# Values turned by VectorE and DRAM instead of TensorE in one stage of a fp32 hybrid layer (1 core)

## The chip, the cores and the metric

One core of one Trainium2 chip runs the whole layer in one launch. The metric is the device time in microseconds (us), the median of the runs. Engines are TensorE (PE, with its weight loads PEld), VectorE (DVE), ScalarE (ACT), GpSimd (POOL) and SyncE (SP, which here only issues DMAs).

## What is computed

One layer on 2048 prompt frames and 8 x 16 sample frames, all in float32. Cut to what the change touches:

```python
h = rmsnorm(x, norm_mix_pre)
P = h @ w_in            # q|k|v (3*512) | z | b | a | B | C | H
qkv = silu(causal_dwconv(qkv_in, conv_prev, conv_qkv_w))
q = l2norm(q) * GDN_HEAD_DIM ** -0.5
k = l2norm(k)
A = strict_lower((k * beta) @ k.T * decay)          # chunks of 64, 4 heads of 128
sol = triangular_solve(eye + A, [v * beta, k * beta * exp(g)])
qk = lower(q @ k.T * decay)
o = ...                 # recurrence over chunks with state S
o = rmsnorm(o, gdn_norm_w) * silu(z)
y = B * causal_dwconv3(C * H)
x = x + rmsnorm(concat(o, y) @ w_o)
x = x + rmsnorm((silu(h @ w_gate) * (h @ w_up)) @ w_down)
```

## The kernel before

The program runs in stages. Stage 1 (0 to about 851 us) is the in-projection with convolution, delta rule and short convolution; then come the out-projection (L1200), gate and up (L1446) and down (L1637). The change lies in stage 1 alone.

Stage 1 takes 17 tiles of 128 rows in five groups: tiles 0 to 3, 4 to 7, 8 to 10, 11 and 12 with the sample tile, and 13 to 15. They are called group 0 to group 4 here ("two to five" in the words of the change are 1 to 4). Each group goes through 28 blocks of 128 output columns: k, v, q, z for four heads, then C, H, B for four slices. A block is 24 matmuls (L326: eight k-slices, each as hi times hi, lo times hi and hi times lo) into one of three `dbank` banks. Weights come block by block, 1 MB each, into one of three buffers; the loads stand in order on SP's queue (`fetch`).

TensorE's order is written by hand. A block has three **slots** (k-slices 0 to 2, 3 to 5, 6 and 7), so a group has 84, and a slot is 9, 9 or 6 matmuls. `plan` hangs all other work on slot numbers through `at(slot, function)`: `SEQS` is the order of the blocks, `PLAN` gives the slots of the decay, the pairs, the solve, the levels and the chunks, `TURNS` the slots of the turns. The other engines' order is made by a scheduler at build time from that program.

The work around the change, by head h and tile i of a group:

- `conv_qkv` evacuates a block, DVE adds three taps (L330), ACT takes silu, and the result stands transposed (head dimension on partitions, tokens along): kT, qT and vraw.
- `turned` (L384) turns it back by one TensorE transpose a tile into a `tbank`. k is copied to `kt` (L409), v is scaled by beta times the norm into `vt` (L427), and of q only the sum of squares is taken (`sumsq`: ACT squares, L389, DVE adds up, L390).
- `pair_keys` (L597) multiplies k by k into a `gbank`, and DVE multiplies that by the decay into AU (L598). `pair_queries` (L604, L605) does the same with q and k.
- `solve_load` copies the 32 x 32 diagonal blocks of AU to `pk` (ACT, L620), turns them to `As` (DVE, L622) and loads half a unit matrix to `Ts` (L612). `solve` then runs 31 dependent steps on DVE (L631, L633), and `solve_store` turns the solved blocks twice (L638 to `td`, L639 to `ud`).
- `level_a` (L650) begins on TensorE with `td`, and `level_b` (L671, L672) and `level_cd` (L699, L701) build the larger inverse; then `chunk` runs the recurrence, from L768 on.
- There are two `gbank` banks, so a matmul that opens one waits until DVE or ACT has emptied the last but one.

## Time and profile before

| | us |
|---|---|
| median of three runs | 2421.25 (2420.97 to 2421.59) |
| the profiled execution | 2421.49 |
| its span in the profile | 2419.5 |

The profile's page gives for the whole span: PE busy 2402.4 us (99%), DVE 1603.4 (66%), ACT 1064.3 (44%), POOL 561.3 (23%), TensorE's granted clock 0.999, DMA 561.36 MB at a mean of 232 GB/s. A table by stretches shows the part in question: between 260 and 850 us PE is busy for 588.7 of 590 us, DVE for 59 to 67 of every 100 us, the DMA engines for 0.58 to 0.76 of the time. Read the table against the page: the span is the time from the first to the last instruction, and the 2.0 us between it and the profiled execution's time lie around the program.

### The profile page before, as it was taken

What the parts mean: (1) busy time and instruction counts of PE and PEld (TensorE: products, weight loads), DVE (VectorE), ACT (ScalarE), POOL (GpSimd) and SP (SyncE); (2) the same over time, 40 slices, a digit from 0 to 9 for tenths busy, and PEclk for the clock granted to TensorE, in tenths of its full rate; (3) what the DMA queues carried; (4) which work ended last, traced back from release to release, by engine and by line L of the source; (5) the groups of instructions that cost most, each with busy time, mean ns of one, the idle gap of its engine ahead of it and who ended that gap; (6) DMA issues with size and microseconds to landing.
All of it is one profiled execution on the core that took longest, in us unless ns stands there. A gap on an engine that the chain in (4) does not pass through costs nothing.

```text
span 2419.5 us, 39078 instructions
## 1 busy us (share of the span) xinstructions
PE 2402.4 (99%) x14222; PEld 2204.9 (91%) x14222; DVE 1603.4 (66%) x3042; ACT 1064.3 (44%) x2367; POOL 561.3 (23%) x667
## 2 busy tenths in 40 slices
PE   9999999999999999999999999999999999999998
PEld 7888889999989988899999999999999988888877
DVE  7875755746667466888788744546456555666787
ACT  6645545546445445543444423334333345333443
POOL 1211001001110000256555200000000035455663
PEclk9999999999999999999999999999999999999999
DMA  8774655766777668599888888888988844334376
GB/s 289 259 245 170 221 192 195 251 216 240 259 260 248 243 177 240 208 339 296 271 280 267 287 254 254 256 261 271 311 297 282 253 154 129 101 120 127 118 235 205
DMA packets 317063, 561.36 MB, mean 232 GB/s; under 512 B 95940, under 2 KB 198536, under 8 KB 299592
## 3 DMA queue, kind: packets, MB, share of 16 engines
q1 hardware_dynamic: 216864, 490.66, 61.1%
q10 hardware_dynamic: 99784, 67.17, 9.0%
q8 instruction: 112, 1.84, 0.3%
q0 software_dynamic: 224, 1.05, 0.1%
q14 instruction: 79, 0.65, 0.1%
HBM read 400.09 MB, written 158.70 MB: 231 GB/s over the span
## 4 chain that ended last, share of the span: by engine, by line
PE 93%; DVE 3%; ACT 1%; DMA 1%; POOL 1%; issue 1%; POOLq 0%; SPq 0%; DVEq 0%; ACTq 0%
PE fbank L1446 36%; PE dbank L326 25%; PE fbank L1637 17%; PE dbank L1200 4%; PE ftbank L1200 4%; PE tbank L384 1%; PE gbank L597 1%; PE gbank L604 1%; PE obank L776 1%; PE gbank L768 1%; PE gbank L790 1%; PE obank L798 1%; PE gbank L784 1%; DVE sA L1413 0%; PE gbank L701 0%
## 5 line engine op out<-in xcount | busy, mean ns | idle before, releaser
L1446 PE MATMUL fbank<-xh,fw 128*128 128x384 f32 (+1 forms) x3696 | 898.2, 326 | 2.7 <-ACT m L1479 1.7
L1446 PEld LDWEIGHTS fbank<-xh,fw 128*128 128x128 f32 x3696 | 651.2, 188 | 5.0 <-ACT m L1478 2.7
L326 PE MATMUL dbank<-hi,w 128*128 128x384 f32 (+1 forms) x2224 | 650.8, 363 | 0.2 <-ACT w L1008 0.2
L1446 PE MATMUL fbank<-xl,fw 128*128 128x384 f32 (+1 forms) x1848 | 602.1, 326 | 0.0
L326 PEld LDWEIGHTS dbank<-hi,w 128*128 128x128 f32 x2224 | 409.6, 188 | 40.4 <-issue 4.5
L1637 PE MATMUL fbank<-dw,as 128*128 128x512 f32 x1785 | 416.1, 391 | 2.5 <-ACT as L1617 1.1
L1637 PEld LDWEIGHTS fbank<-dw,as 128*128 128x128 f32 x1785 | 334.6, 188 | 76.9 <-ACT as L1617 1.5
L326 PE MATMUL dbank<-lo,w 128*128 128x384 f32 (+1 forms) x1112 | 396.7, 357 | 0.3 <-DVE lo L241 0.3
L1446 PEld LDWEIGHTS fbank<-xl,fw 128*128 128x128 f32 x1848 | 346.9, 188 | 0.0
L326 PEld LDWEIGHTS dbank<-lo,w 128*128 128x128 f32 x1112 | 209.3, 188 | 16.0 <-DVE lo L241 0.6
L1620 POOL TENSOR_TENSOR as<-ar,as 128x256 fp32r<-128x256 f32 (+1 forms) x202 | 173.8, 869 | 182.3 <-ACT as L1617 170.4
L1617 ACT CAST as<-ar 128x256 fp32r<-128x256 f32 (+1 forms) x287 | 119.0, 427 | 203.1 <-PE fbank L1637 154.9
L1590 DVE TENSOR_TENSOR acc<-acc,fbank 128x512 f32<-128x512 f32 x219 | 148.0, 683 | 86.7 <-PE fbank L1637 68.5
L1285 POOL TENSOR_TENSOR dw<-dr,dw 128x512 fp32r<-128x512 f32 x48 | 67.7, 1418 | 513.8 <-ACT dw L1283 513.4
L1421 ACT CAST fw<-rg 128x512 fp32r<-128x512 f32 x124 | 77.2, 622 | 223.3 <-PE fbank L1446 136.8
L330 DVE SCALAR_TENSOR_TENSOR acc<-R,vec,acc 128x512 f32<-128x512 f32 (+2 forms) x180 | 120.8, 673 | 26.8 <-ACT acc L367 20.9
L1494 DVE TENSOR_TENSOR c<-u,fbank 128x384 f32<-128x384 f32 (+1 forms) x66 | 34.9, 528 | 98.1 <-PE fbank L1446 98.1
L1490 DVE TENSOR_TENSOR m<-m,m 128x384 f32<-128x384 f32 (+1 forms) x44 | 23.1, 526 | 81.3 <-ACT m L1480 81.2
L1497 ACT ACTIVATE c<-c 128x384 f32<-128x384 f32 (+1 forms) x66 | 33.4, 506 | 95.3 <-DVE c L1496 95.3
L1422 POOL TENSOR_TENSOR fw<-rg,fw 128x512 fp32r<-128x512 f32 x44 | 65.9, 1499 | 34.1 <-ACT fw L1421 34.0
L1492 ACT ACTIVATE m<-fbank 128x384 f32<-128x384 f32 (+1 forms) x66 | 31.2, 473 | 94.0 <-PE fbank L1446 70.2
L359 POOL COPY hist<-R 128x3 f32<-128x3 f32 x60 | 18.4, 307 | 217.9 <-ACT R L335 172.3
(402 smaller groups left out, 3558.2 us busy)
## 6 DMA issues: line engine op xcount, KB each, us to landing
w<-wsplit SPq DMA_DIRECT2D x105, 1024.0 KB, 5.1
fw<-fsplit SPq DMA_DIRECT2D x188, 512.0 KB, 4.8
fsplit<-fw SPq DMA_DIRECT2D x94, 512.0 KB, 4.3
partd<-pt ACTq DMA_DIRECT2D x86, 384.0 KB, 6.3
rg<-in_w_gu SPq DMA_DIRECT2D x62, 512.0 KB, 4.3
wsplit<-w SPq DMA_DIRECT2D x28, 1024.0 KB, 4.9
ar<-partd SPq DMA_DIRECT2D x43, 384.0 KB, 3.2
wr<-in_w_in SPq DMA_DIRECT2D x32, 512.0 KB, 6.2
```

Of the source, the lines that this page charges most:

```text
L326: T.matmul(ps[:, :c], l[:, k, :], r[k][:, :c], start=(k == 0 and r is hi and l is wh), stop=(k == KD - 1 and l is wl))
L330: r = V.scalar_tensor_tensor(acc, raw(d), w[:, d:d + 1], acc, op0=ALU.mult, op1=ALU.add)
L1200: T.matmul(pss[n], m_[:, j, :], w_[k][:, n * 512:(n + 1) * 512], start=(k == 0 and ci == 0), stop=(k == KD - 1 and ci == 2))
L1285: e.tensor_tensor(out=w[1], in0=v, in1=w[0].bitcast(F32), op=ALU.subtract)
L1421: A.copy(w[:, 0], v)
L1422: e.tensor_tensor(out=w[:, 1], in0=v, in1=w[:, 0].bitcast(F32), op=ALU.subtract)
L1446: T.matmul(ps, w_[:, c], b_[k][:, :hw], start=(first and k == 0 and ci == 0), stop=(k == KH - 1 and ci == 2), skip_group_check=not first)
L1494: V.tensor_add(c21, u2, b3)
L1590: mark_d["V"] = V.tensor_tensor(out=dst if out is None else out, in0=dst, in1=ps, op=ALU.add)
L1617: ins = mark_d["A"] = A.copy(a[:, 0, :n], v)
L1620: mark_d["V" if e is V else "G"] = e.tensor_tensor(out=a[:, 1, :n], in0=v, in1=a[:, 0, :n].bitcast(F32), op=ALU.subtract)
L1637: ins = T.matmul(ps, a[:, x_, q * P:(q + 1) * P], w[y_], start=(start and q == 0 and ci == 0), stop=(q == c - 1 and ci == 2), skip_group_c ...
```

## The change

For groups 1 to 4 (group 0 stays as it is):

1. **Values.** The TensorE transposes of v go. DVE transposes vraw within 32 x 32 blocks into `vt` (`turn`), four DMAs a head write it to DRAM in pieces of 128 bytes so that the blocks land where they belong (`turn_out`), one DMA a head reads it back in pieces of 512 bytes (`turn_in`), and ACT scales it in place (`value_scale`). All four have their own slots in `TURNS`.
2. **Queries.** The TensorE transposes of q go. DVE turns qT within 32 x 32 blocks, ACT squares, DVE adds up 32 columns at a time to four parts, and four small matmuls with 32 x 32 unit matrices (`eyes`) add the four parts (`query_sums`), which DVE copies out. The turn of q is held behind `leveled`, an instruction of `level_b`.
3. **Order.** The blocks go k, v, z, q instead of k, q, z, v; so `pair_queries` moves from slot 42 to 62 in group 1 and from 33 to 53 in the others. Its multiply is held behind `solved` (the second turn in `solve_store`). The chunks of group 1 begin at slot 68 instead of 66.
4. **Unit matrix.** The load of half a unit matrix moves 14 slots ahead.

```diff
@@ -37,17 +37,20 @@
 AX = mybir.AxisListType
 BLOCKS = [(kind, h) for kind in "kvqz" for h in range(H)] + [(kind, b) for b in range(4) for kind in "CHB"]
 SEQS = ([0, 12, 1, 13, 2, 14, 3, 15, 8, 16, 9, 17, 10, 4, 11, 5, 18, 6, 19, 7, *range(20, 28)],
-        [16, 17, 18, *range(0, 4), *range(8, 12), *range(12, 16), *range(4, 8), *range(19, 28)],
-        [*range(0, 4), *range(8, 12), *range(12, 16), *range(4, 8), *range(16, 28)])
+        [16, 17, 18, *range(0, 8), *range(12, 16), *range(8, 12), *range(19, 28)],
+        [*range(0, 8), *range(12, 16), *range(8, 12), *range(16, 28)])
 LATE = (*SEQS[0][:2], 7, 11, 19, 23, 27)
 PLAN = {0: (14, 20, 22, 26, 32, 36, 40, 50, (67, 69, 71), 75),
-        1: (16, 20, 23, 28, 26, 33, 38, 51, (56, 58, 60), 66),
+        1: (16, 20, 23, 28, 26, 33, 38, 51, (56, 58, 60), 68),
         2: (8, 14, 17, 22, 17, 28, 32, 47, (52, 55, 58), 63),
         3: (8, 14, 17, 22, 17, 28, 32, 47, (53, 56, 59), 64),
         4: (8, 14, 17, 22, 17, 28, 32, 47, (52, 55, 57), 62)}
-TURNS = ({"k": (19, 19, 31, 31), "q": (43, 43, 55, 55), "v": (52, 52, 64, 64)},
-         {"k": (17, 20, 23, 26), "q": (33, 33, 39, 39), "v": (55, 55, 61, 61)},
-         {"k": (14, 14, 17, 17), "q": (28, 28, 31, 31), "v": (46, 46, 52, 52)})
+TURNS = ({"k": ((19,), (19,), (31,), (31,)), "q": ((43,), (43,), (55,), (55,)), "v": ((52,), (52,), (64,), (64,))},
+         {"k": ((17,), (20,), (23,), (26,)), "v": ((29, 30, 37, 50), (32, 35, 42, 54), (35, 41, 48, 58), (38, 47, 54, 64)),
+          "q": ((62, 64), (63, 65), (64, 66), (65, 67))},
+         {"k": ((14,), (14,), (17,), (17,)), "v": ((20, 21, 28, 44), (23, 27, 34, 48), (26, 33, 40, 54), (29, 39, 46, 59)),
+          "q": ((57, 59), (58, 60), (59, 61), (60, 62))})
+QSUM = (0, 69, 64)
 TLS = True
 O_SPLIT = 7
 NPD, NPT, NPG = 3, 2, 2
@@ -129,6 +132,7 @@
     mixo = [dram.tile([P, H, P], F32, name=f"mixo{t}") for t in range(NT)]
     mixs = [dram.tile([P, 4, len(g) * P], F32, name=f"mixs{gi}") for gi, g in enumerate(GROUPS)]
     wsplit = [dram.tile([P, 2, KD, P], F32, name=f"wsplit{j}") for j in range(28)]
+    turnd = [dram.tile([H, len(g) * P, P], F32, name=f"turn{gi}") for gi, g in enumerate(GROUPS)]
     hTd = [dram.tile([4 * len(g), 32, D] if gi else [D, len(g) * P], F32, name=f"hTd{gi}") for gi, g in enumerate(FGROUPS)]
     partd = [[dram.tile([len(g) // 2, P, 7, len(c) // 2, P], F32, name=f"partd{gi}_{ch}") for ch, c in enumerate(FCHUNKS)]
              for gi, g in enumerate(FGROUPS)]
@@ -390,6 +394,47 @@
             V.tensor_reduce(out=ss[:, :4 * n].rearrange("p (t h) -> p h t", h=H)[:, h], in_=sq[:, :n * P].rearrange("p (t d) -> p t d", d=P),
                             axis=AX.X, op=ALU.add)
 
+        def turn(g, h, src):
+            V.transpose(g["vt"][:, h, :g["n"]].rearrange("p t d -> p (t d)"), src[:, :g["n"] * P])
+
+        def turn_out(g, h):
+            n, v = g["n"], g["vt"][:, h]
+            for a in range(4):
+                r = slice(32 * a, 32 * a + 32)
+                with tc.issue_after(wloads[-1].ins):
+                    nc.sync.dma_start(out=turnd[g["gi"]][h, :, r].rearrange("(j c) f -> c j f", c=32),
+                                      in_=v[r, :n].rearrange("c t (j f) -> c (t j) f", f=32))
+
+        def turn_in(g, h):
+            with tc.issue_after(wloads[-1].ins):
+                nc.sync.dma_start(out=g["vt"][:, h, :g["n"]], in_=turnd[g["gi"]][h].rearrange("(t p) d -> p t d", p=P))
+
+        def query_squares(g, h, src):
+            c = g["n"] * P
+            qb = g["qb", h] = cp.tile([P, W1], F32, tag="vraw", name="qb", bufs=NKV)
+            with tc.issue_after(g["leveled"].ins):
+                V.transpose(qb[:, :c], src[:, :c])
+            A.activation(qb[:, :c], qb[:, :c], AF.Square)
+
+        def query_parts(g, h):
+            c = g["n"] * P
+            if not h:
+                g["pq"] = small.tile([P, 4, MAXT, H], F32, tag="pq", name="pq", bufs=1)
+            V.tensor_reduce(out=g["pq"][:, :, :g["n"], h].rearrange("p j t -> p t j"),
+                            in_=g["qb", h][:, :c].rearrange("p (t j f) -> p t j f", j=4, f=32), axis=AX.X, op=ALU.add)
+
+        def query_sums(g):
+            m = 4 * g["n"]
+            ps = bank()
+            for j in range(4):
+                T.matmul(ps[32 * j:32 * j + 32, :m], eyes, g["pq"][:, j, :g["n"]].rearrange("p t h -> p (t h)"), start=True, stop=True)
+            V.tensor_copy(g["ssq"][:, :m], ps[:, :m])
+
+        def value_scale(g, h):
+            for i in range(g["n"]):
+                v = g["vt"][:, h, i]
+                A.activation(v, v, AF.Copy, scale=g["rt"][:, 4 * i + h:4 * i + h + 1])
+
         def sm(nm, w=4 * MAXT):
             return small.tile([P, w], F32, tag=nm, name=nm)
 
@@ -407,7 +452,7 @@
                     tb, t3 = turned(o, n)
                     sumsq(tb, n, g["ssk"], h)
                     A.copy(g["kt"][:, h, :n], t3)
-                return later
+                return [later]
             if kind == "q":
                 o = gp.tile([P, W1], F32, tag="qT", name="qT", bufs=H)
                 conv_qkv(tiles, h, ps, o, rb)
@@ -416,7 +461,7 @@
                 def later():
                     tb, _ = turned(o, n)
                     sumsq(tb, n, g["ssq"], h)
-                return later
+                return [lambda: query_squares(g, h, o), lambda: query_parts(g, h)] if g["gi"] else [later]
             if kind == "v":
                 raw = cp.tile([P, W1], F32, tag="vraw", name="vraw", bufs=NKV)
                 conv_qkv(tiles, 8 + h, ps, raw, rb)
@@ -425,7 +470,10 @@
                     _, t3 = turned(raw, n)
                     for i in range(n):
                         A.activation(g["vt"][:, h, i], t3[:, i], AF.Copy, scale=g["rt"][:, 4 * i + h:4 * i + h + 1])
-                return later
+                if g["gi"]:
+                    return [lambda: turn(g, h, raw), lambda: turn_out(g, h), lambda: turn_in(g, h),
+                            lambda: value_scale(g, h)]
+                return [later]
             if kind == "z":
                 src = ps[:, :c]
                 if rb is not None:
@@ -602,14 +650,17 @@
             ps = bank()
             for h in range(H):
                 T.matmul(ps[:, h * P:(h + 1) * P], g["kT"][h][:, c], g["qT"][h][:, c], start=True, stop=True)
-            V.tensor_mul(g["dt"][:, i], h4(ps), g["dt"][:, i])
+            with tc.issue_after(g["solved"].ins) if g["gi"] else ExitStack():
+                V.tensor_mul(g["dt"][:, i], h4(ps), g["dt"][:, i])
+
+        def solve_eye(g):
+            g["Ts"] = wk.tile([P, 1024], F32, tag="Ts", name="Ts")[:, :512]
+            with tc.issue_after(wloads[-1].ins):
+                nc.sync.dma_start(out=g["Ts"], in_=half_eye)
 
         def solve_load(g):
-            n = g["n"]
-            As, Ts = (wk.tile([P, 1024], F32, tag=nm, name=nm) for nm in ("As", "Ts"))
-            Ts = Ts[:, :512]
-            with tc.issue_after(wloads[-1].ins):
-                nc.sync.dma_start(out=Ts, in_=half_eye)
+            n, Ts = g["n"], g["Ts"]
+            As = wk.tile([P, 1024], F32, tag="As", name="As")
             pk = wk.tile([P, H, P], F32, tag="kl", name="pk").rearrange("p h c -> p (h c)").rearrange("p (i x) -> p i x", i=32)
             if n < MAXT:
                 G.memset(pk, 0.0)
@@ -636,7 +687,7 @@
             utd = wk.tile([P, 1024], F32, tag="As", name="utd")
             ud, td = (utd[:, 512 * q:512 * q + 512].rearrange("p (x c) -> p x c", c=32) for q in range(2))
             V.transpose(td.rearrange("p x (k e) -> p k e x", e=2), g["Ts"].rearrange("p i c -> p c i"))
-            V.transpose(ud, td)
+            g["solved"] = V.transpose(ud, td)
             g.update(ud=ud.rearrange("p (t h) c -> p t h c", h=H), td=td.rearrange("p (t h) c -> p t h c", h=H))
 
         def level_a(g):
@@ -675,7 +726,7 @@
                 r1, r2 = slice(b, b + 32), slice(b + 32, b + 64)
                 V.tensor_scalar_mul(U[r1, :npr, :, r2], p4(r1), -1.0)
                 if b == 0:
-                    V.tensor_scalar_mul(AU[r2, :npr, :, r1], p4(r2), -1.0)
+                    g["leveled"] = V.tensor_scalar_mul(AU[r2, :npr, :, r1], p4(r2), -1.0)
             G.memset(AU[0:32, :npr, :, 32:64], 0.0)
 
         LO, HI = slice(0, 64), slice(64, 128)
@@ -884,7 +935,10 @@
                 at(mask + i, decay_mask, g, i)
                 at(pairs + 3 * (i // 2) + i % 2 - 1, decay_scale, g, i)
                 at(pairs + 3 * (i // 2), pair_keys, g, i)
-                at((52, 42, 33)[min(gi, 2)] + 3 * (i // 2), pair_queries, g, i)
+                at((52, 62, 53)[min(gi, 2)] + 3 * (i // 2), pair_queries, g, i)
+            at(load - (14 if gi else 0), solve_eye, g)
+            if gi:
+                at(QSUM[min(gi, 2)], query_sums, g)
             at(load, solve_load, g)
             for b in range(4):
                 at(load + 2 + 3 * b * (store - load - 2) // 13, solve, g, range(8 * b, min(31, 8 * b + 8)))
@@ -1048,6 +1102,10 @@
         shist = gp.tile([P, 4, 2], F32, name="shist")
         G.memset(hist, 0.0)
         G.memset(shist, 0.0)
+        eyes = gp.tile([P, 32], F32, name="eyes")
+        for b in range(4):
+            r = slice(32 * b, 32 * b + 32)
+            G.tensor_copy(eyes[r], ident[r, r])
         nega = gp.tile([P, 4], F32, name="nega")
         with tc.issue_after(held[0].ins):
             A.activation(nega, vec[:, 141:145], AF.Exp)
@@ -1104,10 +1162,9 @@
                     if not early:
                         matmuls(ps, w, hi, lo, c, ks)
                     if s == 2:
-                        later = finish_block(j, ps, g)
-                        if later:
-                            kind, h = BLOCKS[j]
-                            events.setdefault(TURNS[min(gi, 2)][kind][h], []).insert(0, later)
+                        kind, h = BLOCKS[j]
+                        for t, f in zip(TURNS[min(gi, 2)].get(kind, ((),) * 4)[h], finish_block(j, ps, g) or ()):
+                            events.setdefault(t, []).insert(0, f)
                         if gi or slot not in (2, 3):
                             with tc.issue_after(mark["rb"].ins), tc.issue_after(mark["E"].ins) if not gi and slot < 2 else ExitStack():
                                 fetch()
```

In what follows a build lists each engine's instructions in their order. After the change the lines of the file are numbered higher: L330 is the block matmul on PE, L334 a tap of a convolution on DVE.

**PE in group 2, around `level_a`.** Before (L384 is the turn of the last head's values, L650 `level_a`):

```order
L326 MATMUL dbank<-hi,w_4965 128x384 x2
L326 MATMUL dbank<-lo,w_4965 128x384
L326 MATMUL dbank<-hi,w_4965 128x384
L384 MATMUL tbank<-cst,vraw 128x128 x6
L650 MATMUL gbank<-utd,AU 32x32 x24
L326 MATMUL dbank<-hi,w_4965 128x384
L326 MATMUL dbank<-lo,w_4965 128x384
L326 MATMUL dbank<-hi,w_4965 128x384 x2
```

After (L701 is `level_a`, L652 `pair_queries`):

```order
L330 MATMUL dbank<-lo,w_4947 128x384
L330 MATMUL dbank<-hi,w_4947 128x384
L701 MATMUL gbank<-utd,AU 32x32 x24
L330 MATMUL dbank<-hi,w_4947 128x384
L330 MATMUL dbank<-lo,w_4947 128x384
L330 MATMUL dbank<-hi,w_4947 128x384 x2
L330 MATMUL dbank<-lo,w_4947 128x384
L330 MATMUL dbank<-hi,w_4947 128x384
L652 MATMUL gbank<-qT,kT 128x128 x8
L330 MATMUL dbank<-hi,w_4991 128x384
```

The six transposes ahead of `level_a` are gone, and `pair_queries` of the first two tiles, which stood some 80 block matmuls ahead of it, now stands a slot behind it. Group 4 reads alike.

**PE and DVE in group 3, around `level_a`.** PE before:

```order
L326 MATMUL dbank<-hi,w_6708 128x384
L384 MATMUL tbank<-cst,vraw 128x128 x6
L326 MATMUL dbank<-hi,w_6708 128x384
L326 MATMUL dbank<-lo,w_6708 128x384
L326 MATMUL dbank<-hi,w_6708 128x384 x2
L326 MATMUL dbank<-lo,w_6708 128x384
L326 MATMUL dbank<-hi,w_6708 128x384
L650 MATMUL gbank<-utd,AU 32x32 x16
L326 MATMUL dbank<-hi,w_6766 128x384
L326 MATMUL dbank<-lo,w_6766 128x384
```

PE after:

```order
L330 MATMUL dbank<-lo,w_6693 128x384
L330 MATMUL dbank<-hi,w_6693 128x384
L652 MATMUL gbank<-qT,kT 128x128 x8
L701 MATMUL gbank<-utd,AU 32x32 x16
L330 MATMUL dbank<-hi,w_6741 128x384
L330 MATMUL dbank<-lo,w_6741 128x384
```

DVE before (L638 and L639 are the turns to `td` and `ud`, L450 and L456 evacuate a block of the short convolution):

```order
L631 TENSOR_TENSOR pr<-As,Ts 128x16
L633 TENSOR_TENSOR Ts<-Ts,pr 128x16
L638 STREAM_TRANSPOSE utd<-Ts 128x32x16
L639 STREAM_TRANSPOSE utd<-utd 128x512
L450 TENSOR_TENSOR u<-cs,dbank 128x256
L456 TENSOR_TENSOR u<-cs,dbank 128x8x16
L660 COPY U<-utd 32x12x32 x4
L457 COPY sch<-u 128x16
```

DVE after (L689 and L690 are the turns to `td` and `ud`, L498 and L504 the same evacuation, L654 the multiply of `pair_queries`):

```order
L498 TENSOR_TENSOR u<-cs,dbank 128x256
L504 TENSOR_TENSOR u<-cs,dbank 128x8x16
L682 TENSOR_TENSOR pr<-As,Ts 128x16
L505 COPY sch<-u 128x16
L684 TENSOR_TENSOR Ts<-Ts,pr 128x16
L689 STREAM_TRANSPOSE utd<-Ts 128x32x16
L334 SCALAR_TENSOR_TENSOR acc<-u,vec,acc 128x400
L690 STREAM_TRANSPOSE utd<-utd 128x512
L654 TENSOR_TENSOR dt<-gbank,dt 128x512 x2
```

In this group alone `pair_queries` stands right ahead of `level_a` on PE, and on DVE its multiplies stand behind both turns; the evacuation, which stood behind the turns, now stands ahead of the last step of the solve, and a tap stands between the turns.

**DVE in group 1, around the third level.** Before (L709 empties the bank of `level_cd`, L306 splits a weight row):

```order
L676 TENSOR_SCALAR U<-gbank 32x16x32
L678 TENSOR_SCALAR AU<-gbank 32x16x32
L676 TENSOR_SCALAR U<-gbank 32x16x32
L450 TENSOR_TENSOR u<-cs,dbank 128x512
L709 TENSOR_SCALAR U<-gbank 64x8x64
L306 TENSOR_TENSOR w_3543<-wr,w_3543 128x1024
L330 SCALAR_TENSOR_TENSOR acc<-u,vec,acc 128x512 x2
L283 TENSOR_TENSOR xk<-xk,rb 128x384
```

After (L310 is the split, L654 the multiply of `pair_queries`; on PE eight L652, the matmuls of `pair_queries`, stand directly ahead of the first L752 of `level_cd`):

```order
L416 STREAM_TRANSPOSE qb<-qT 128x512 x2
L423 TENSOR_REDUCE pq<-qb 128x4x4 x2
L416 STREAM_TRANSPOSE qb<-qT 128x512 x2
L423 TENSOR_REDUCE pq<-qb 128x4x4 x2
L498 TENSOR_TENSOR u<-cs,dbank 128x512
L654 TENSOR_TENSOR dt<-gbank,dt 128x512
L310 TENSOR_TENSOR w_3497<-wr,w_3497 128x1024
L334 SCALAR_TENSOR_TENSOR acc<-u,vec,acc 128x512
L654 TENSOR_TENSOR dt<-gbank,dt 128x512
L334 SCALAR_TENSOR_TENSOR acc<-u,vec,acc 128x512
L287 TENSOR_TENSOR xk<-xk,rb 128x384
L760 TENSOR_SCALAR U<-gbank 64x8x64
```

The multiplies of `pair_queries` come between the evacuation L498 and the taps, with the weight split and a tap between the two of them, where before DVE emptied the bank of `level_cd` right behind the evacuation.

## Rows read from the trace of the kernel before

**Rows 1.** The page, part 1: busy time, share of the span, instructions.

```profile
PE 2402.4 (99%) x14222; PEld 2204.9 (91%) x14222; DVE 1603.4 (66%) x3042; ACT 1064.3 (44%) x2367; POOL 561.3 (23%) x667
```

**Rows 2.** The page, part 4: the chain that ended last, by engine.

```profile
PE 93%; DVE 3%; ACT 1%; DMA 1%; POOL 1%; issue 1%; POOLq 0%; SPq 0%; DVEq 0%; ACTq 0%
```

**Rows 3.** That chain in time order, group 1: start us, us, what.

```profile
284.78 0.87 PE tbank L384 x8
```

**Rows 4.** The chain, group 3, two small matmul pairs.

```profile
570.48 0.12 PE gbank L527 x2
570.61 0.22 PE gbank L528 x2
```

**Rows 5.** The chain, group 2, from pairs to level_a.

```profile
442.67 1.79 PE gbank L597 x16
...
450.19 2.62 PE dbank L326 x15
...
482.69 0.67 PE tbank L384 x6
483.36 0.07 issue
483.43 0.95 PE gbank L650 x47
```

**Rows 6.** DVE's timeline, group 2: start us, us, engine, line, out<-in, count.

```profile
450.46 0.68 DVE L598 TENSOR_TENSOR AU<-gbank,dt 128x512 f32<-128x512 f32 x1
...
455.20 2.09 DVE L622 STREAM_TRANSPOSE As<-pk 128x1024 f32<-128x1024 f32 x1 [3.91 <-ACT pk L620]
457.13 1.27 DVE L605 TENSOR_TENSOR dt<-gbank,dt 128x512 f32<-128x512 f32 x2
...
482.14 1.14 DVE L638 STREAM_TRANSPOSE utd<-Ts 128x512 f32<-128x512 f32 x1
```

**Rows 7.** ACT's timeline in the same stretch.

```profile
451.68 3.49 ACT L620 COPY pk<-AU 32x384 f32<-32x384 f32 x4
457.32 1.28 ACT L736 ACTIVATE kl<-kt,tl 128x128 f32<-128x128 f32 x4 [2.16 <-DVE As L622]
```

**Rows 8.** The chain, group 4.

```profile
755.23 2.62 PE dbank L326 x15
...
788.40 0.05 issue
```

**Rows 9.** The chain, group 3, last pair_keys to level_a.

```profile
600.34 2.62 PE dbank L326 x15
...
634.55 0.62 PE gbank L650 x32
```

**Rows 10.** DVE's timeline, group 3.

```profile
633.73 0.71 DVE L639 STREAM_TRANSPOSE utd<-utd 128x512 f32<-128x512 f32 x1
634.66 0.42 DVE L450 TENSOR_TENSOR u<-cs,dbank 128x256 f32<-128x256 f32 x1 [0.22 <-PE dbank L326]
```

**Rows 11.** DVE's timeline, group 1.

```profile
337.13 0.69 DVE L450 TENSOR_TENSOR u<-cs,dbank 128x512 f32<-128x512 f32 x1 [7.56 <-PE dbank L326]
...
338.74 1.21 DVE L306 TENSOR_TENSOR w<-wr,w 128x1024 fp32r<-128x1024 f32 x1
339.87 1.52 DVE L330 SCALAR_TENSOR_TENSOR acc<-u,vec,acc 128x512 f32<-128x512 f32 x2
```

**Rows 12.** DMA issues: out<-in, engine, operation, count, KB each, us to landing.

```profile
w<-wsplit SPq DMA_DIRECT2D x105, 1024.0 KB, 5.1
...
hTd<-ht SPq DMA_DIRECT2D x24, 128.0 KB, 4.3
```

**Rows 13.** The page, part 2: mean busy share of the DMA engines, 40 slices of the span.

```profile
DMA  8774655766777668599888888888988844334376
```

**Rows 14.** Stretches: busy of PE, PEld, DVE, ACT, POOL; PEclk, DMA share, GB/s.

```profile
885.00:895.00 10.00, 10.00 (x45) 8.23 (x44) 6.49 (x12) 3.69 (x10) 1.10 (x2) 1.00 0.79 202
...
935.00:945.00 10.00, 10.00 (x46) 8.19 (x45) 3.25 (x7) 2.43 (x8) 0.99 (x2) 1.00 0.98 347
```

## Prediction

> **What bounds the kernel now.** The page's first part comes first: PE is busy for 99% of the span, every other engine has a third or more to spare [rows 1]. The chain of waits, which follows the end of the program back, says the same in another way: 93% of it is PE's own work [rows 2]. So an operation taken off PE in stage 1 is worth its whole time, unless PE then meets something that isn't ready yet. The next view is therefore that chain in order of time, around `level_a`, the place where PE takes up what DVE's solve has made. In group 2 the last six transposes of v end at 483.36, 0.07 us follow that nothing explains, and `level_a` starts at 483.43 [rows 5]. DVE's timeline shows why: the turn to `td` runs from 482.14 for 1.14 us, to 483.28 [rows 6]. `level_a` starts 0.15 us after `td` is there, so PE and DVE arrive together. Group 4 has the same small gap [rows 8]. From the last `pair_keys` to `level_a` the two engines run beside each other, and DVE's side has nothing left. That is what the change meets.
>
> **What goes.** In groups 1 to 4 the transposes of q and v: 13 tiles times 4 heads times 2 are 104. The chain gives 0.87 us for eight [rows 3] and 0.67 for six [rows 5], 0.11 each, so 104 x 0.109 = **-11.4 us**.
>
> **What comes to PE.** `query_sums`: four matmuls a group, which the trace would count as two instructions each. No row shows them; two small matmuls on a `gbank` take 0.12 us in one line and 0.22 in the next [rows 4], so eight instructions cost 0.5 or 0.9; `level_a`'s little ones take 0.95 for 47, 0.02 each [rows 5], a lower end of 0.2. I take 0.5 (they are short in columns, like the first of the two lines), **+2.0 us** for four groups, between 0.6 and 3.5. `pair_queries` is moved, not changed, 16 instructions in the 1.79 us that `pair_keys` takes for as many [rows 5]. PE's own work thus falls by 9.4 us. The rest is waiting.
>
> **Groups 2 and 4, `level_a`.** Count from X, the end of the last `pair_keys` on PE (450.19 in group 2, 755.23 in group 4) [rows 5, 8]. PE reaches `level_a` at X + 33.17 now in group 2. Of that, twelve transposes of v (1.33) go, and `pair_queries` of three tiles (24 instructions, 2.68) stands behind `level_a` afterwards. PE is there at X + 29.2.
> DVE: the multiply to AU starts at 450.46 and takes 0.68, to 451.14 [rows 6]; ACT's copy `pk` starts at 451.68 and takes 3.49, since a `silu` stands ahead of it [rows 7]. The new order of ACT has that `silu` behind `pk`, so `pk` can start at X + 1.0 and end at X + 4.5. From the turn to As (455.20) to `td` (483.28) are 28.1 us [rows 6], with three multiplies of `pair_queries` in them: 1.27 for two [rows 6], 1.8 by their starts for all. These are held behind the solve now, which leaves 26.3. The convolution taps between the steps are as many as before. So `td` is ready at X + 30.8, 2.3 us earlier than today, but PE comes 4 us earlier. PE waits 30.8 + 0.15 - 29.2, some **1.7 us, in each of the two groups, less the 0.1 of today: +3.2**. Bounds: nothing if the scheduler's cover holds better than I read, 3.4 each if the next evacuation slips in ahead of `td` as it does in group 3.
>
> **Group 3.** Here `pair_queries` of two tiles stands directly ahead of `level_a`, and `level_a` needs the bank that DVE's multiply empties. PE gets from 600.34 to 634.55 in 34.2 us now [rows 9]; without twelve transposes (1.3) and without 24 instructions, but with 16 back (1.79), it is ready at X + 32.0. On DVE the evacuation of the short convolution now stands ahead of the last solve step. It waits for its PE block: today it starts at 634.66 [rows 10], 34.3 after X, and the block comes 4 us earlier, X + 30.3. Behind it: 0.6 for the two evacuations, 0.5 for the last step and a copy, 1.14 for the turn to `td` (price of [rows 6]), a tap of about 0.65, 0.71 for the turn to `ud` [rows 10], 0.68 for the multiply: X + 34.6. PE waits **+2.6 us**; bounds 0 and 3.5. It gains 3.3 of transposes less 0.5, so this group comes out even.
>
> **Group 1.** The solve has time here. But the matmuls of `pair_queries` (1.79) stand right ahead of `level_cd`, whose first matmul needs the bank of the second multiply. DVE's order behind the block's end is: evacuation 0.69, multiply 0.68, weight split 1.21, tap 0.76 [rows 11], multiply 0.68, in all 4.0, and 0.2 for the two handovers. PE is there after 1.8: **+2.4 us**; bounds 1.0 (if the split runs ahead) and 3.0.
>
> **Work that I cost at nothing.** DVE gets eight turns and four adds a group, each like the 0.71 of a 128 x 512 turn [rows 10]; it is a third idle [rows 1], and turns of q are held until `level_b` is through. If that cover goes, `query_sums` comes late, and PE waits at it; it stands some slots ahead of the first user. ACT loses its copies out of the transposes' banks and gains scales in place. The load of the unit matrix was early enough and is earlier. The spread-out transfers: 64 of 48 or 64 KB in pieces of 128 bytes. The nearest row is `hTd`, which writes 128 KB in such pieces and lands after 4.3 us [rows 12]. Even if nothing overlapped, the 3.4 MB would be 26 of those, 112 us of the 590; by the rate while they run (202 GB/s at a share of 0.79, against 347 at 0.98 afterwards [rows 14]) they are 13 us. The DMA engines have 0.2 to 0.4 of their time free there in slices 5 to 14 [rows 13]. I take them as hidden. The weights behind them on SP's queue land in 5.1 us [rows 12] and are asked for two blocks, over 8 us, ahead; the cover is 3 us.
>
> [...]
>
> **The sum.** -11.4 + 2.0 + 3.2 + 2.6 + 2.4 = -1.2 us against the profiled execution's 2421.49, so 2420.3; the median lies 0.24 below that execution: **2420.0 us**. Its own range, with the waits between their bounds but not all at one end, is 2416.8 to 2423.
>
> **Rivals.**
> 1. *The gain goes through.* If PE's waits are small, because DVE runs ahead of where the order suggests or because the bank is free earlier, up to 9.4 us remain: 2412 us; half of the waits gives 2416. For it: PE is the bound by every view, and DVE has a third free. Against: the 0.15 us between `td` and `level_a` in two groups, which leave nothing. Chance 0.32.
> 2. *Weights come late.* A `turn_in` waits on SP for its own four writes, with the next weight loads behind it. If it holds the queue for 3 us more than the cover in a group, PE waits that long: 2423. Chance 0.07.
> 3. *Values come late, slower than before.* In groups 2 to 4 the scale of head 0's values stands ahead of `pk` on ACT. Its `turn_in` is issued about when the first `pair_keys` runs (442.67 [rows 5]), lands 4.3 us later at 447.0, the three scales take 0.3 each (four tail keys take 1.28 [rows 7]), and `pk` is wanted at 451.1: the cover is 3.1 us. From there each microsecond of lateness delays `pk`, the solve and `level_a` in three groups. The change is slower by over 0.2% from 2.0 us past the cover, a landing of some 9.4 us instead of 4.3. At 2.5 us past it: 2420.0 + 7.5 = 2427.5. For it: four writes and a read in a row through DRAM. Against: seven slots, some 10 us, lie between the writes and the read. Chance 0.09.
>
> **How the numbers follow.** A measurement of this kernel tells about 0.2% (4.8 us) from no change, so faster is below 2416.4 and slower above 2426.1. The forecast has 0.52, nearly all within. Rival 1 is faster in most of its cases (0.30 of 0.32), to which 0.02 of the forecast's lower tail come: 0.32. Rival 3 gives 0.09 slower, and rival 2 with everything dearer at once another 0.02. Left for the same: 0.57. The range reaches into rival 1 to 2412.5, short of the whole gain, and to 2425.5 above; about 2 in 10 are outside, a part of the first rival and the slower ones.
>
> **What would show it.** Right: no L384 on q or v in groups 1 to 4; a wait of 1 to 2 us ahead of `level_a` in groups 2 and 4, released by the turn to `td`; one of 2 to 3 us there in group 3 and ahead of the first `level_cd` in group 1, released by the multiply of `pair_queries`; PE's busy time lower by some 9 us and the span by 1. Wrong: `level_a` following its block without a gap (rival 1), gaps of L330 released by a DMA (rival 2), or `pk` waiting for the scales of v (rival 3).

## The result and the profile after

The changed kernel takes 2428.86 us (2424.02 to 2429.98, seven runs) against 2421.04 for the kernel before, a ratio of 1.0028 (95% interval 1.0018 to 1.0037). It is slower by 7.8 us where 1.2 faster was forecast. The profiled execution took 2425.91 us, the shortest but one, so its profile shows 4.9 of the 7.8 us; a second profile of the same kernel, below, took 2429.77.

The page's first part, and the chain by engine, of the changed kernel:

```profile
PE 2397.8 (99%) x14150; PEld 2199.7 (91%) x14150; DVE 1619.6 (67%) x3078; ACT 1069.2 (44%) x2367; POOL 565.6 (23%) x671
```

```profile
PE 91%; DVE 3%; DMA 2%; ACT 2%; issue 1%; POOL 1%; SPq 0%; POOLq 0%; DVEq 0%; ACTq 0%
```

PE is busy for 4.6 us less than before [rows 1], and its share of the chain is down by two points [rows 2]. PE's waits in stage 1 (who waited, for whom, us in total, times, the longest):

```profile
PE gbank L701 <- DVE utd L689: 3.7, 2, 2.3
PE gbank L701 <- DVE dt L654: 2.5, 1, 2.5
PE gbank L750 <- DVE dt L654: 2.0, 1, 2.0
```

All four are new, and they stand where the prediction put them. `level_a` waits for `td` in groups 2 and 4 (3.7 in two, the longer 2.3) and for a multiply of `pair_queries` in group 3 (2.5); the third level of group 1 waits for such a multiply too (2.0). Together 8.2 us, as forecast. That alone would leave the kernel a little faster than before. What the prediction didn't have shows in a table of stretches (from:to, length, busy us of PE, PEld, DVE, ACT, POOL, then TensorE's granted clock, the DMA share and GB/s):

```profile
330.00:334.00 4.00, 2.06 (x19) 1.80 (x17) 3.74 (x6) 1.67 (x2) 0.18 (x1) 1.00 0.12 51
334.00:340.00 6.00, 5.91 (x56) 4.79 (x57) 2.46 (x5) 1.20 (x2) 0.35 (x1) 1.00 0.34 141
477.00:480.00 3.00, 0.69 (x15) 0.40 (x14) 2.71 (x9) 1.40 (x4) 0.00 (x0) 1.00 0.69 266
480.00:486.00 6.00, 6.00 (x67) 5.94 (x63) 3.82 (x8) 3.77 (x9) 0.59 (x2) 0.50 0.57 169
...
633.00:636.00 3.00, 0.55 (x5) 0.36 (x4) 2.79 (x5) 1.11 (x3) 0.00 (x0) 1.00 0.76 255
636.00:641.00 5.00, 4.97 (x48) 4.93 (x49) 3.18 (x12) 2.98 (x8) 1.34 (x3) 0.66 0.61 218
641.00:646.00 5.00, 5.00 (x92) 4.84 (x91) 3.84 (x9) 0.00 (x0) 0.72 (x3) 1.00 0.43 111
```

The clock is the third number from the right. In 477 to 480 PE is busy for 0.69 of 3 us, the wait of group 2. In the next 6 us it is busy throughout, **at a granted clock of 0.50**. A fall stands behind the wait of group 3 too (636 to 641, a mean of 0.66). Behind group 1's wait (330 to 334) the clock stays at 1.00. The chain shows what that does to the work (start us, us, what):

```profile
448.40 13.54 PE dbank L330 x78
...
478.62 1.09 DVE utd L689
...
479.85 1.40 PE gbank L701 x47
481.25 2.22 PE dbank L330 x6
483.47 3.41 PE gbank L652 x16
```

Sixteen instructions of `pair_queries` take 3.41 us here; sixteen of the like took 1.79 [rows 5]. Summed over stretches of 1 us, the two falls cost 3.4 and 1.7 us, 5.1 together.

| | out-projection begins | gate and up take | time of that execution |
|---|---|---|---|
| before | 851.9 | 916.4 | 2421.49 |
| after | 854.6 | 917.5 | 2425.91 |
| after, second profile | 853.3 | 923.1 | 2429.77 |

(First starts of the out-projection's and of gate and up's matmuls, and from there to the first of down.) Stage 1 can be added up: -11.4 for the transposes, +0.7 for `query_sums`, +8.2 of waits less the 0.1 of before, +5.1 for the clock, in all +2.5; measured 854.6 - 851.9 = +2.7. The stretches check it without a forecast term: from 60 us to the out-projection PE is busy for 789.96 us before and 785.22 after, 4.7 less, or 9.8 less with the clock's 5.1 taken out; it idles for 1.9 before and 9.4 after.

Stage 1 thus explains +2.7 in the first profile and +1.4 in the second. The rest, 1.1 and 6.7 us, is lost in gate and up; in the second profile, whose time is near the median, that is the larger part.

### The profile page after: what moved, and what is told of

It reads as the page before. It is cut to its first block, busy times and chain, and to the rows that moved or that the text cites. A ratio compares the mean times of both kernels' runs of the same rounds, so it can differ in the third digit from the quotient of the medians.

```text
span 2423.7 us, 39091 instructions
## 1 busy us (share of the span) xinstructions
PE 2397.8 (99%) x14150; PEld 2199.7 (91%) x14150; DVE 1619.6 (67%) x3078; ACT 1069.2 (44%) x2367; POOL 565.6 (23%) x671
## 4 chain that ended last, share of the span: by engine, by line
PE 91%; DVE 3%; DMA 2%; ACT 2%; issue 1%; POOL 1%; SPq 0%; POOLq 0%; DVEq 0%; ACTq 0%
PE fbank L1503 37%; PE dbank L330 23%; PE fbank L1694 17%; PE dbank L1257 4%; PE ftbank L1257 4%; DMA xt<-in_x 1%; PE gbank L645 1%; PE gbank L652 1%; DMA wr<-in_w_in 1%; PE gbank L819 1%; PE obank L827 1%; PE gbank L841 1%; PE gbank L835 1%; PE obank L849 1%; DVE acc L334 0%
## 5 line engine op out<-in xcount | busy, mean ns | idle before, releaser
L330 PE MATMUL dbank<-hi,w 128*128 128x384 f32 (+1 forms) x2224 | 651.0, 363 | 0.2 <-ACT w L1062 0.2
L330 PEld LDWEIGHTS dbank<-hi,w 128*128 128x128 f32 x2224 | 411.3, 189 | 41.0 <-issue 3.6
L330 PE MATMUL dbank<-lo,w 128*128 128x384 f32 (+1 forms) x1112 | 397.7, 358 | 0.0
L330 PEld LDWEIGHTS dbank<-lo,w 128*128 128x128 f32 x1112 | 210.0, 189 | 15.9 <-DVE lo L245 0.5
L334 DVE SCALAR_TENSOR_TENSOR acc<-R,vec,acc 128x512 f32<-128x512 f32 (+2 forms) x180 | 120.2, 669 | 27.1 <-ACT acc L371 22.7
```

Of the source, the lines that this page charges most:

```text
L330: T.matmul(ps[:, :c], l[:, k, :], r[k][:, :c], start=(k == 0 and r is hi and l is wh), stop=(k == KD - 1 and l is wl))
L334: r = V.scalar_tensor_tensor(acc, raw(d), w[:, d:d + 1], acc, op0=ALU.mult, op1=ALU.add)
```

## The experiments

Theory A: the waits cost their length, and behind a wait the clock may fall, which costs about as much again (5.1 us behind the waits of 2.3 and 2.5 us in groups 2 and 3); the gain of the transposes is real. Theory B: the spread-out transfers are the cause, through other loads that land late. Theory C came later: what stage 1 gains, PE waits for again in part where gate and up begin.

**e1_no_waits.** Waits designed away.

```diff
-        2: (8, 14, 17, 22, 17, 28, 32, 47, (52, 55, 58), 63),
+        2: (8, 14, 17, 22, 17, 26, 30, 47, (52, 55, 58), 63),
...
-                at((52, 62, 53)[min(gi, 2)] + 3 * (i // 2), pair_queries, g, i)
+                at((52, 66, 53, 54, 53)[gi] + 3 * (i // 2), pair_queries, g, i)
```

(Groups 3 and 4 in the same way.)

> The changed kernel with its waits designed away: pairs and solve two slots earlier in groups 2 to 4, pair_queries behind level_a in group 3 and behind the third level in group 1. [...] Theory B (the spread-out transfers hold up other loads, the rows of x above all, and DVE and ACT come late whatever the slots are): waits of 1 us and more remain, 2418 to 2427 us.

Measured 2415.84 us (2413.35 to 2418.67), ratio to before 0.9982 (0.9972 to 0.9992): 13 us less than the change with the same work on PE, and 2 to 5 above the 2411 to 2414 that Theory A gave. The granted clock is 1.00 in every microsecond of stage 1, as Theory A had it; the stage ends at 844.1. `level_a` and the third level no longer wait; a wait of pairs, 2.4 us in three places, is new:

```profile
PE gbank L645 <- DVE AU L646: 2.4, 3, 1.1
```

The repeated times spread over 5 us, where Theory A gave 1. In gate and up this profile has a wait of 1.8 us that ends at 1321, and a granted clock of 0.57 in the 4 us behind it.

**e2_before_wait.** The kernel before with `level_a` one and two slots earlier, so that it must wait, and nothing else.

```diff
-        2: (8, 14, 17, 22, 17, 28, 32, 47, (52, 55, 58), 63),
+        2: (8, 14, 17, 22, 17, 28, 32, 47, (51, 55, 58), 63),
...
-        4: (8, 14, 17, 22, 17, 28, 32, 47, (52, 55, 57), 62)}
+        4: (8, 14, 17, 22, 17, 28, 32, 47, (50, 55, 57), 62)}
```

> The kernel before with nothing but level_a moved ahead of work that hid the solve, by one slot in group 2 and by two in group 4, so PE must wait some 2.2 and some 3.8 us there. Waiting alone: 2421 + 6 = 2427 us with a granted clock of 1.00 throughout stage 1. [...] Theory B says nothing on it beyond the waits: 2427 us.

Measured 2430.1 us (2429.1 to 2431.31), ratio 1.0040 (1.0025 to 1.0055): 9.5 us lost, where the waits are 2.2 and 3.8 us. The stretches of the waits, and of the work behind them:

```profile
482.00:484.00 2.00, 0.62 (x39) 0.65 (x41) 1.91 (x3) 0.55 (x2) 0.00 (x0) 1.00 0.94 374
484.00:486.00 2.00, 2.00 (x29) 1.96 (x22) 1.66 (x4) 1.56 (x4) 0.41 (x1) 0.86 0.70 253
486.00:489.00 3.00, 3.00 (x13) 2.90 (x13) 0.00 (x0) 2.07 (x7) 0.00 (x0) 0.53 0.04 14
...
788.00:792.00 4.00, 0.34 (x2) 0.02 (x1) 3.55 (x14) 0.90 (x2) 0.00 (x0) 1.00 0.92 261
792.00:796.00 4.00, 3.89 (x57) 3.86 (x58) 2.32 (x5) 1.96 (x4) 0.54 (x1) 0.58 0.50 180
```

The mean clock is 0.53 in 486 to 489, behind the first wait, and 0.58 in 792 to 796, behind the second, and this costs 3.4 us in sum, by stretches of 1 us. 6.0 + 3.4 = 9.4. PE's busy time says the same: from 60 us to the out-projection it is 793.31 us against 789.96 in the kernel before, 3.4 more for the same instructions. So the fall comes behind a wait without any part of the change; the longer wait's fall costs no more than the shorter one's, 1.7 us each where Theory A gave 3 or more, and the time stayed just under the 2431 to 2435 us that it gave.

**e9_fill.** The changed kernel with useless work where PE waited.

```diff
+        def fill(g, m):
+            ps = tbank()
+            for i in range(m):
+                T.transpose(ps[:, :P], g["kT"][i % H][:, :P], ident)
...
+            if gi > 1:
+                at(a, fill, g, (0, 0, 20, 22, 12)[gi])
             at(a, level_a, g)
...
+                if gi == 1 and step == 1:
+                    at(t, fill, g, 18)
                 at(t, level_cd, g, step)
```

> The changed kernel with useless transposes of k into a spare bank at the four places where PE waits: 18 in group 1, 20, 22 and 12 in groups 2 to 4, 72 x 0.109 = 7.8 us of added work on PE that nobody reads. [...] If the loss were waiting alone: no gain, 2428 to 2431 us.

Measured 2420.85 us (2419.44 to 2422.48), ratio to before 1.0002 (0.9993 to 1.0011); Theory A, with PE at work where it idled, gave 2421 to 2425. **72 more transposes make the kernel 7 to 8 us faster than the change** (2428.86 above, 2428.16 in e10_after_again). On PE's timeline the fill stands between the block and `level_a` (L706), which waits 0.56 us more, and in the stretches the clock doesn't move:

```profile
477.29 2.34 PE L388 MATMUL tbank<-cst,kT 128*128 128x128 f32 x20
480.19 0.95 PE L706 MATMUL gbank<-utd,AU 32*32 32x32 f32 x48 [0.56 <-DVE utd L694]
```

```profile
476.00:480.00 4.00, 3.63 (x29) 3.36 (x27) 3.59 (x13) 1.36 (x4) 0.00 (x0) 1.00 0.97 350
480.00:486.00 6.00, 5.81 (x82) 5.80 (x83) 5.56 (x13) 3.81 (x9) 0.74 (x3) 1.00 0.63 217
...
634.00:640.00 6.00, 6.00 (x98) 5.84 (x98) 4.59 (x16) 2.27 (x6) 1.39 (x4) 1.00 0.40 145
```

This is the cleanest of the runs: the change is kept as a whole, its transfers too, and only PE's work in the waits is added. Nearly the whole loss goes, that in gate and up as well (916.4 us in this profile, as before); by what path idling in stage 1 reaches gate and up, no run shows.

**e4_banks.** `pair_queries` alone moved (the second edit of e1_no_waits).

> The changed kernel with pair_queries alone moved, behind level_a in group 3 and behind the third level in group 1, so that no bank is waited for; level_a still comes early in groups 2 and 4. Theory A: the waits of groups 1 and 3 (2.0 and 2.5 us) go and with them one or two falls of the clock; group 2 keeps its wait and its fall: 2417 to 2423 us. Theory B: no fewer than 2423 us, since the late rows of x stay.

Measured 2424.07 us (2416.54 to 2425.75), ratio 1.0012 (1.0003 to 1.0021): outside Theory A's range and inside Theory B's. The waits of the banks went, but in group 3 others took their place:

```profile
PE gbank L701 <- DVE utd L689: 6.2, 3, 2.6
...
PE gbank L722 <- DVE dt L654: 1.3, 1, 1.3
```

`level_a` now waits for `td` in three groups, 6.2 us, and level_b of group 3 for the multiply, 1.3. The bank had hidden that `td` was late in group 3 as well. It is not Theory B's lateness: DVE's only idling in that solve is 1.1 us ahead of the evacuation L498, which waits for PE's block.

**e3_no_dma.** The changed kernel without `turn_out` and `turn_in`: the values stay where DVE's turn left them.

```diff
         def turn_out(g, h):
-            n, v = g["n"], g["vt"][:, h]
...
+            pass
...
         def turn_in(g, h):
-            with tc.issue_after(wloads[-1].ins):
...
+            pass
```

> The changed kernel without the transfers of turn_out and turn_in: the values are not brought back to their places, so the recurrence is computed from wrongly placed values; all other work is as in the changed kernel. Theory A: the waits of PE stay (the bank waits of groups 1 and 3 at 2.0 and 2.5 us, level_a in groups 2 and 4 at 1.4 to 2.3 us) and so do the clock's falls, 2424 to 2430 us. Theory B: the rows of x land in some 5 us instead of 7 to 8, the waits at level_a shrink below 1.5 us, 2419 to 2422 us.

Measured 2422.1 us (2417.46 to 2426.74), ratio to before 1.0005 (0.9995 to 1.0015), between the two expectations. The waits stay, those at `level_a` a little shorter:

```profile
PE gbank L696 <- DVE utd L684: 3.0, 2, 1.5
PE gbank L696 <- DVE dt L649: 2.1, 1, 2.1
PE gbank L745 <- DVE dt L649: 2.0, 1, 2.0
```

Those for `td` fall from 3.7 to 3.0: group 2's goes from 2.3 to 1.5 us. The falls of the clock stay at 5.1 us, now three of them. Theory B has its share: in the changed kernel a load of x rows for the next group takes 7.06 us in group 2 (5.36 here, though the one issued right behind it still takes 6.99), ACT stands behind it in its queue, and DVE idles 0.80 us in the middle of the solve, which it doesn't here. The chain's row, and DVE's timeline:

```profile
462.82 7.06 DMA xt<-in_x
```

```profile
472.25 0.62 DVE L334 SCALAR_TENSOR_TENSOR acc<-R,vec,acc 128x384 f32<-128x384 f32 x1 [0.80 <-ACT acc L371]
```

In stage 1 the transfers thus cost a longer wait. That is not the whole of the 6 to 7 us by which this run is faster than the change: the waits are 1.1 us shorter, the clock costs as much, and stage 1 ends 2.0 and 0.7 us earlier than in the change's two profiles. The rest lies in gate and up (916.4 us here); whether the transfers or chance made that, no run decides.

**e10_after_again.** The changed kernel, another execution's profile.

> The changed kernel itself once more, for a profile of another execution. [...] If the times differ by the waits: the waits differ by microseconds.

Measured 2428.16 us (2425.23 to 2430.93), the profiled execution 2429.77. Theory A gave the same four waits within 0.3 us, and one to four falls behind them that would make the difference in time. In stage 1 the four waits differ from the first profile by 0.4 us at most, the falls cost 5.1 us again. The other 5 us are not in stage 1: gate and up take 923.1 us. Its stretches there:

```profile
1046.00:1050.00 4.00, 2.32 (x14) 2.00 (x13) 3.02 (x6) 1.90 (x4) 2.57 (x3) 1.00 0.98 338
1070.00:1073.00 3.00, 1.12 (x6) 0.80 (x6) 2.41 (x6) 1.51 (x3) 0.59 (x1) 0.99 1.04 402
1073.00:1077.00 4.00, 4.00 (x15) 4.00 (x15) 1.18 (x3) 1.00 (x2) 3.03 (x3) 0.58 1.03 397
...
1333.00:1335.00 2.00, 0.01 (x1) 0.01 (x1) 1.90 (x4) 1.78 (x4) 0.00 (x0) 1.00 0.77 262
1335.00:1340.00 5.00, 5.00 (x20) 5.00 (x21) 3.58 (x4) 3.77 (x8) 4.42 (x4) 0.66 0.85 283
```

PE waits at the start of gate and up (1046 to 1050, 1070 to 1073) and once more at 1333, and behind two of these waits the clock falls (means of 0.58 in 1073 to 1077 and 0.66 in 1335 to 1340): 3.4 us for the clock. All this is code that the change doesn't touch. PE idles there for 6.8 us in all, against 2.7 before and 4.0 in the first profile. The DMA share is 0.98 and more where gate and up begin, but so it is in the kernel before (1.00 from 1045 to 1049, with PE busy throughout).

**e5_best.** Decay and mask one slot earlier than in e1_no_waits.

```diff
-        2: (8, 14, 17, 22, 17, 26, 30, 47, (52, 55, 58), 63),
+        2: (8, 14, 16, 21, 17, 26, 30, 47, (52, 55, 58), 63),
```

> The kernel of e1_no_waits with decay and mask one slot earlier in groups 2 to 4, since pair_keys waited there for 2.4 us in three places. Theory A: no wait over 0.5 us in stage 1, clock 1.00 there, 2411 to 2414 us. If the pairs' wait has another cause than the decay: 2415 to 2417 us as in e1_no_waits.

Measured 2417.38 us (2415.94 to 2420.58), ratio 0.9989 (0.9980 to 0.9999). A miss: the pairs wait as long as before, 2.6 us, so the mask's slot is not what they wait for. What it is stayed open.

**e6_best_no_dma.** e5_best without the transfers (edit of e3_no_dma).

> e5_best without the transfers of turn_out and turn_in (the values are not brought back to their places). Theory A: the transfers cost something only where they lengthen a wait of PE; without waits nothing is left, within 1.5 us of e5_best. Theory B: the transfers slow other loads and with them later work, 3 to 6 us below e5_best.

Measured 2415.29 us (2410.79 to 2415.67), 2.1 us below e5_best, between the two expectations; stage 1 ends 0.4 us earlier. It doesn't decide.

**e11_fill_end.** e1_no_waits with useless work at the end of stage 1.

```diff
+            if gi == 4:
+                at(80, fill, g, 70)
             at(a, level_a, g)
```

> e1_no_waits with 70 useless transposes of k (7.6 us) near the end of stage 1, so that PE comes to the out-projection as late as in the kernel before. Theory C (what stage 1 gains, PE partly waits for again where gate and up begin, since the DMA engines, busy for 0.98 of the time there, are no earlier than before): gate and up take 916.5 us as before instead of 918.4, and the time is 2420 to 2422 us, 5 to 6 above e1_no_waits and not 7.6. If the handover depends on something else that the change brought: 2423 to 2425 us, 7.6 above.

Measured 2420.91 us (2420.1 to 2422.06): 5.1 above e1_no_waits for 7.6 us of added work, and the spread is down from 5 to 2 us. Gate and up take 915.9 us in its profile, 918.4 in that of e1_no_waits, as Theory C forecast. But the place isn't Theory C's. PE's waits in gate and up, in e1_no_waits and then here:

```profile
PE fbank L1503 <- ACT m L1535: 2.1, 2, 1.8
PE fbank L1503 <- ACT m L1536: 1.9, 1, 1.9
```

```profile
PE fbank L1510 <- ACT m L1543: 1.7, 1, 1.7
PE fbank L1510 <- ACT m L1542: 0.8, 4, 0.2
```

Some 28 us into gate and up both wait alike, 1.9 and 1.7 us. The difference is the wait of 1.8 in e1_no_waits that ends at 1321, 290 us into gate and up, and 1.7 us for the clock behind it. A wait of 1.8 to 2.3 us at that place stands in five of the twelve profiles, of kernels that come to the out-projection early (e1_no_waits, e5_best, e12_pairs) and late (e4_banks, e10_after_again), and in only one of the two of the change. So Theory C isn't shown.

**e12_pairs.** e1_no_waits with pairs and solve one slot later (27 and 31 in place of 26 and 30).

> e1_no_waits with pairs and solve one slot later again in groups 2 to 4 (one slot ahead of the change's). Theory A: pair_keys' wait of 2.4 us in all goes to under 0.5, level_a waits 0.5 to 1.2 us in groups 2 and 4, too short for the clock to fall; 2414 to 2416 us. [...]

Measured **2414.03 us** (2411.2 to 2420.18), ratio to before 0.9977 (0.9967 to 0.9986): 14.8 us below the change, and the only kernel here with all of the layer's work that is faster than before by over 0.2%. The wait of the pairs is gone, `level_a` waits 1.1 us in two places, and no fall follows in stage 1 (granted clock 1.00 in every microsecond of it):

```profile
PE gbank L701 <- DVE utd L689: 1.1, 2, 0.8
```

## Why the prediction was wrong

- **Transposes, -11.4: right.** Stage 1 of e12_pairs ends 8.9 us before that of the kernel before: from 60 us on PE is busy for 780.16 us against 789.96, 9.8 less, and idle for 0.9 more. The forecast of PE's own work, transposes and `query_sums` together, was 9.4 less.
- **`query_sums`, +2.0: too much.** Eight instructions take 0.18 us, the lower end of the bounds (chain, changed kernel):

```profile
353.35 0.18 PE gbank L430 x8
```

- **The waits: right in place and nearly in size.** Group 1 2.0 (2.4 forecast), group 3 2.5 (2.6), groups 2 and 4 2.3 and 1.4 (1.7 each); in sum 8.2 as forecast. X is 448.40 in group 2, and `td` was ready at X + 31.3, 0.5 later than forecast; e3_no_dma, where the rows of x land sooner, has 1.5 us there. That group 3 would come out even was a slip outside the sum: its 24 transposes are 2.6 us, not 3.3.
- **"PE waits" was priced at its length: this is the step that failed.** The sum has no term for the clock. Two falls in stage 1 cost 5.1 us in each of the two profiles of the change; e2_before_wait shows the fall without the change, e9_fill the change without the fall. Of the 9.0 us between forecast and median, that is over half; `query_sums` takes 1.3 back. So a wait can cost more than its length: group 2's 2.3 us were followed by a fall that cost 3.4, group 3's 2.5 by one that cost 1.7. The trace of before gave no warning: it holds, past the program's start, one wait of 1.4 us or more only (1.7 us, L1446), with no fall behind it. In the changed kernel's stretches of 1 us (474 to 494 and 632 to 645) the granted clock is 0.50 or 1.00, but where a fall begins or ends inside one (0.51, 0.58, 0.78).
- **The rest of the span, costed at nothing: wrong, and the second step that failed.** Gate and up lost 1.1 us in one profile of the change and 6.7 in the other, 3.4 of the 6.7 by the clock again and the rest by PE's waits for a bank that ACT empties. e9_fill brings it back to 916.4 together with the filled waits of stage 1. It does not follow from when PE comes there: e2_before_wait comes latest of all (860.9) and takes 916.2. The cause stays open.
- **Rivals.** The first, a gain that goes through, is what e1_no_waits and e12_pairs are, once the waits are away: it needed other slots. The third was right about slower, by a wrong mechanism: the scales of head 0's values ended before `pk` could start, by 2.7 us in group 2 and 1.5 and 1.8 in groups 3 and 4, and `pk` waited for AU (ACT's timeline, group 2):

```profile
445.52 0.99 ACT L436 ACTIVATE vt<-vt,rt 128x128 f32<-128x128 f32 x3 [0.60 <-DMA vt<-turn]
449.17 3.54 ACT L671 COPY pk<-AU 32x384 f32<-32x384 f32 x4 [2.66 <-DVE AU L646]
```

  The second didn't come: no matmul waited for a weight load. The range ended at 2425.5, 3.4 short, since no bound in it had the clock or gate and up.

## What to carry to other kernels

Where PE is busy for 99% of the span, taking work off it only pays if the next thing that it needs is ready sooner too; count what DVE's chain allows before counting the transposes. Price a new wait of PE of 1.4 us or more at its length and, as seen here, up to 3.4 us again for the clock (past the program's start, 17 of the 38 such waits in the twelve profiles were followed by a fall), and look at the granted clock in stretches of 1 us behind it. If a wait can't be moved away, useless work in it may be cheaper than idling (e9_fill: 2420.85 us against 2428.86), and better still is to move what is waited for: earlier pairs and later `pair_queries` turned +7.8 us into -4.8 and, one slot further on, into -6.6.

## What was not expected of the hardware

- The clock fell about when PE resumed or up to 2 us later, not earlier in the wait. In the changed kernel PE resumes at 479.85 in group 2, and 480 to 481 has 0.51; in group 3 it resumes at 636.03, 636 to 637 still has 1.00 and 637 to 638 has 0.51. In e2_before_wait PE is back before 484, and from 484 to 486 the mean is still 0.86.
- Behind waits of nearly the same length the clock fell or didn't. 2.0 us in group 1: no fall in the three profiles that have it. 1.4 us in group 4: no fall in the change's two profiles, one each in e3_no_dma and e4_banks. Waits of 2.2 us are on record both ways (e4_banks, group 3: none; e10_after_again, group 2: a fall). Waits under 1.4 us had none in any of the twelve profiles, unless a longer one stood close by. The falls lasted 3 to 7 us (in the changed kernel some 6.8 and 3.4). What decides was not settled.
- The clock goes with the times of the change's runs. Of thirteen, the three with a mean granted clock of 0.998 took 2424.0 to 2426.6 us, the two with 0.997 2425.9 and 2426.8, and the eight with 0.996 or 0.995 2427.0 to 2430.9; 0.002 of 2425 us are 4.9. In e9_fill, whose waits are filled, all have 0.998 or 0.999, and the spread is 3 us against 6. It isn't all of the spread in every kernel: e12_pairs has 0.998 or 0.999 in all its runs, which spread over 9 us.
